# An encoder layer in split fp32: residual stage and first row of block products rearranged

## The chip, the cores and the metric

The kernel runs on one core of one Trainium2 chip. The metric is the device time of one execution in microseconds; the median of several executions is given. Engines are named as the profile names them: PE is TensorE's matmul, PEld its weight load, DVE is VectorE, ACT is ScalarE, POOL is GpSimd, SP is the sync engine, which here only issues transfers.

## The reference

One layer on x of 512 positions by 2048 channels, in fp32. Two mixers run on the normalised input, their outputs are concatenated and multiplied by `W_out`, and then the second half of the layer follows:

```python
x = x + rms_norm(concat(A, B) @ W_out, post_gain)         # residual 1
h = rms_norm(x, pre2_gain)
gate, val = split(causal_depthwise_conv(h @ W_up, conv_w), 2)   # three taps
x = x + rms_norm((gelu(gate) * val) @ W_down, post2_gain)
```

The change touches what lies between `concat(A, B) @ W_out` and the products with `W_up`.

## The kernel before

Activations are held transposed: channels on the 128 partitions, 512 positions along the row, so 2048 channels are 16 tiles of 128x512, indexed k. fp32 precision is kept by splitting every operand into a rounded part h (cast on ACT) and the remainder l (a subtraction on DVE); a product is then three matmuls, wh·xh, wh·xl and wl·xh. Weights arrive as `wraw` tiles of 128x1024 (512 KB, SP's queue, three buffers); ACT makes `wh` (L100) and DVE makes `wl` (L101), two buffers each in the pool `wp`. In `gemm` one weight tile feeds 24 matmuls of 512 columns, and eight such tiles (kc = 0 to 7) make one product with all 2048 channels.

The stretch in question, in program order:

- **Residual stage (L679 to L702).** `yt(k)` holds the mixer output, 16 tiles that lie in the two large buffers `yo` (in the rows these show as `s`). All 16 tiles of x were loaded earlier as `xin`. For each k, DVE multiplies `yt(k)` by the norm factor `ry` (L688), DVE adds the product to `xin` (L689), ACT makes the h part (L690), DVE the l part (L691), SP stores the sum to the scratch `x1scr` (L693), ACT squares it (L698), GpSimd adds the square to `ssq` (L699). ACT also writes the sum times its gain back into `yt(k)` (L702), for the block products later. The multiplication of k waits in order for the l part of k-3 (`issue_after`).
- **up(0) and up(1) (L735 to L746).** Two plain products of 2048 channels. PE starts on k = 0 while the residual stage runs, so the matmuls of up(0) follow the l parts. Where up(0) ends, DVE evacuates it (L741, four tiles, scaled by `r2`), scales the block operands by `r2` (L752, four large operations), runs the taps (L728) and forms the block operands (`xsum` L762, `xsplit` L767 to L771).
- **Rows of block products (L793 to L872).** Forty rows f. Each is a 2x2 block product done with seven products instead of eight: sums of weight blocks times sums of input blocks, 24 matmuls of 256 columns each. `quad_load` fetches the weight blocks. Two of them are sums, `s1` and `s3`: SP loads one block, and a transfer issued on GpSimd with `accum_op=ADD` adds the second (L820, L821). `s1`, `s3` and `rb` (block w22) come from the pool `sp`, which is opened where the pool of `yo` was closed and takes its place in memory; so the first loads into `sp` wait until the last reader of `yo`, the split "22" (L770, L771), is done. PE begins the first row with `product(s1, "t1")`.
- **down (from L906).** The product with `W_down`, whose inputs `hidh` (ACT) and `hidl` (DVE) are split in `fload`.

Instructions are put in order per engine by a list scheduler that goes by priority: program order, moved ahead by `tc.high_priority` with WPRI for weight work, EPRI for evacuations, and back with LPRI.

Of the kernel before, what the change touches and what calls it, by code (L numbers as in the profile page):

```python
# [10 lines left out]
F32 = mybir.dt.float32  # L11
I32 = mybir.dt.int32
F32R = mybir.dt.float32r
AF = mybir.ActivationFunctionType
ALU = mybir.AluOpType

P = 128
S = 512
D = 2048
DK = D // P  # L20
# [13 lines left out]
WPRI = 4000  # L34
# [3 lines left out]
LPRI = 30000  # L38
NP = 4
HS = S // 2  # L40

MAGIC = 12582912.0

# [11 lines left out]
MUL, ADD, SUB = ALU.mult, ALU.add, ALU.subtract  # L55
# [3 lines left out]
def layer_kernel(ctx, tc, a, out):  # L59
    nc = tc.nc  # L60
    ve, se, ge, pe, sy = nc.vector, nc.scalar, nc.gpsimd, nc.tensor, nc.sync
# [5 lines left out]
    wp = ctx.enter_context(tc.tile_pool(name="wp", side="right", bufs=2))  # L67
# [159 lines left out]
    g2 = cload("pre_ffn_g", [P, DK])  # L227
# [171 lines left out]
    for h in range(2):  # L399
        wc = s16.tile([P, 2, 16, P], F32, name="s16") if h == 0 else cv.tile([P, 2, 16, P], F32, name="csb")  # L400
        btw.append(wc)
        for j in range(T):
            sy.dma_start(out=wc[j:P:T],
                         in_=wscr[h][:, :, T - 1 - j, :].unsqueeze(0).broadcast_to([HC, 2, 16, P]))
        for mm in range(4):
            m = 4 * h + mm
# [13 lines left out]
    for m in range(8):  # L420
# [15 lines left out]
        for gg in range(2):  # L436
            sy.dma_start(out=cscr[m][:, :, gg].rearrange("r p q t -> p r q t"),
                         in_=ct[PH * gg:PH * gg + PH].rearrange("p r q t h -> p r q (t h)"))
# [44 lines left out]
    for ri in range(2):  # L483
        sy.dma_start(out=bst[PH * ri:PH * ri + PH, :, 0:NQ, :],
                     in_=bscr.rearrange("(g p) r q h -> r p g q h", p=PH)[ri])
# [95 lines left out]
    for m in range(8):  # L581
# [3 lines left out]
                         in1=yh[:, m, :].bitcast(F32).rearrange("p (c j) -> p c j", j=T), op=SUB)  # L585
# [6 lines left out]
    for g in range(2):  # L592
        ps = gemm(a["w_glu"][g], yrhs)
        for i in range(4):
            m = 4 * g + i
            with tc.high_priority(offset=EPRI):
# [4 lines left out]
                             in1=sg.rearrange("p (c j) -> p c j", j=T), op=MUL)  # L601
# [13 lines left out]
    for i in range(8):  # L615
# [3 lines left out]
        else:  # L619
            sq = tmp()  # L620
# [13 lines left out]
    xin = ExitStack()  # L634
    xip = xin.enter_context(tc.tile_pool(name="xin", bufs=1, reuse_waits="tile"))
    x1s = []
    for k in range(DK):
        x1 = xip.tile([P, S], F32, name=f"xin{k}")
        sy.dma_start(out=x1, in_=a["x"][:, k, :])
        x1s.append(x1)  # L640
# [4 lines left out]
    def yt(m):  # L645
        return yo[m // 8][:, m % 8, :]
# [10 lines left out]
    for g in range(4):  # L657
        ps = gemm(a["w_out"][1, g], crhs)
        for i in range(4):
            m = 4 * g + i  # L660
            with tc.high_priority(offset=EPRI if m < DK - 1 else LPRI):
                ve.tensor_tensor(out=yt(m), in0=ps[i], in1=yt(m), op=ADD)
                sq = yss if m == 0 else tmp()
# [8 lines left out]
    ry = rsqrt_bcast([yss] + last, D, False)  # L672
# [7 lines left out]
    xadds, xls = [], []  # L680
    xs2 = rp.tile([P, S], F32, name="ssq")
    for k in range(DK):
        x1 = x1s[k]
        h, l = hrhs[k]
        with ExitStack() as order:
            if k:
                order.enter_context(tc.issue_after(xadds[k - 1] if k < 3 else xls[k - 3]))
            ve.tensor_tensor(out=yt(k), in0=yt(k), in1=ry, op=MUL)  # L688
        xadds.append(ve.tensor_tensor(out=x1, in0=x1, in1=yt(k), op=ADD).ins)  # L689
        se.activation(out=h, in_=x1, func=AF.Copy, scale=g2[:, k:k + 1])  # L690
        xls.append(ve.scalar_tensor_tensor(out=l, in0=x1, scalar=g2[:, k:k + 1], in1=h.bitcast(F32),  # L691
                                           op0=MUL, op1=SUB).ins)
        sy.dma_start(out=x1scr[:, k, :], in_=x1)  # L693
        if k == 0:
            se.activation(out=xs2, in_=x1, func=AF.Square)
        else:
            sq = tmp()
            se.activation(out=sq, in_=x1, func=AF.Square)  # L698
            ge.tensor_tensor(out=xs2, in0=xs2, in1=sq, op=ADD)  # L699
    r2 = rsqrt_bcast([xs2], D)  # L700
    for k in range(DK):
        se.activation(out=yt(k), in_=x1s[k], func=AF.Copy, scale=g2[:, k:k + 1])  # L702
    xin.close()


    upx = ExitStack()
    xt = upx.enter_context(tc.tile_pool(name="xt", bufs=1, reuse_waits="tile"))
    tset = [[xt.tile([P, 8, HS], F32R, name=f"t{i}{p}") for p in "hl"] for i in range(3)]
    NA = 4
    abuf = [xt.tile([P, S + 2], F32, name=f"ab{i}") for i in range(NA)]  # L710
    for t in abuf:
# [37 lines left out]
    for i in range(2):  # L749
        for j in range(2):  # L750
            o = slice(HS * j, HS * j + HS)
            ve.tensor_tensor(out=yo[i][:, :, o], in0=yo[i][:, :, o],  # L752
                             in1=r2[:, o].unsqueeze(1).broadcast_to([P, 8, HS]), op=MUL)
    q11, q12 = yo[0][:, :, 0:HS], yo[0][:, :, HS:S]
# [9 lines left out]
    def xsplit(name, src, sign=1.0):  # L764
        h, l = xset[name]
        if sign > 0:
            se.copy(out=h, in_=src)  # L767
            ve.tensor_tensor(out=l, in0=src, in1=h.bitcast(F32), op=SUB)
        else:
            se.activation(out=h, in_=src, func=AF.Copy, scale=-1.0)  # L770
            ve.scalar_tensor_tensor(out=l, in0=src, scalar=-1.0, in1=h.bitcast(F32), op0=MUL, op1=SUB)  # L771
# [10 lines left out]
    for i in range(1, NP // 2):  # L782
        up(i)
    xsplit("11", q11)
    xsplit("21", q21)
    xsplit("t4", q12)
    xsplit("22", q22, -1.0)
    s16x.close()

# [2 lines left out]
    sp = spx.enter_context(tc.tile_pool(name="sp", side="right", bufs=1, reuse_waits="tile"))  # L792
    nw = [0]  # L793

    def product(raw, name, ps, first, last):
        pool = sp if nw[0] % 3 == 2 else wp
        nw[0] += 1
        h = pool.tile([P, 1024], F32R, name="wh")
        l = pool.tile([P, 1024], F32R, name="wl")
        with tc.high_priority(offset=WPRI):  # L800
            se.copy(out=h, in_=raw)  # L801
            ve.tensor_tensor(out=l, in0=raw, in1=h.bitcast(F32), op=SUB)  # L802
        h, l = (v.rearrange("p (k f) -> p k f", f=P) for v in (h, l))
        xh_, xl_ = xset[name]
        o = ps[:, 0:HS]
        for k in range(8):
            pe.matmul(o, h[:, k, :], xh_[:, k, :], start=first and k == 0, stop=False, skip_group_check=True)  # L807
            pe.matmul(o, h[:, k, :], xl_[:, k, :], start=False, stop=False, skip_group_check=True)  # L808
            pe.matmul(o, l[:, k, :], xh_[:, k, :], start=False, stop=last and k == 7, skip_group_check=True)  # L809

    def quad_load(f):
        src = a["ffn_w_quad"][f - NP]
        with tc.high_priority(offset=WPRI):
            s1 = sp.tile([P, 1024], F32, name="s1", bufs=2)
            sy.dma_start(out=s1, in_=src[2])
            s3 = sp.tile([P, 1024], F32, name="s3", bufs=2)
            sy.dma_start(out=s3, in_=src[0])
            w11 = wp.tile([P, 1024], F32, name="wraw", bufs=3)
            sy.dma_start(out=w11, in_=src[0])
            ge.dma_start(out=s1, in_=src[3], accum_op=ADD)  # L820
            ge.dma_start(out=s3, in_=src[2], accum_op=ADD)  # L821
            w12 = wp.tile([P, 1024], F32, name="wraw", bufs=3)
            sy.dma_start(out=w12, in_=src[1])
            w22 = sp.tile([P, 1024], F32, name="rb", bufs=2)
            sy.dma_start(out=w22, in_=src[3])
        return w11, w12, s3, w22, s1
# [14 lines left out]
    for f in range(NP, NFF):  # L841
        ws = quad_load(f)
        w11, w12, s3, w22, s1 = ws
# [51 lines left out]
    def fload(b):  # L895
        r = []
        for i in range(4):
            if b:
                t = hid.tile([P, S], F32, name="fin", bufs=6)
                sy.dma_start(out=t, in_=fscr[:, 4 * b + i, :])  # L900
            else:
                t = f0[i]
            h = hid.tile([P, S], F32R, name="hidh")
            se.copy(out=h, in_=t)  # L904
            l = hid.tile([P, S], F32R, name="hidl")
            ve.tensor_tensor(out=l, in0=t, in1=h.bitcast(F32), op=SUB)  # L906
            r.append((h, l))
        return r

# [113 lines left out]
```

## Time and profile before

| | us |
|---|---|
| median of 3 runs | 2112.39 |
| lowest and highest | 2111.09, 2114.02 |
| profiled execution, its own time | 2115.38 |
| span of the profiled execution | 2112.5 |
| PE busy | 1962.2 (93%) |
| DVE busy | 1518.5 (72%) |
| ACT busy | 829.3 (39%) |
| POOL busy | 364.9 (17%) |
| mean granted TensorE clock | 0.964 |

PE is busy for 93% of the span, so what a change can win lies in PE's pauses and in the stretches where the clock is at its lower level. The list of waits names each pause by the PE instruction that waited, the instruction that ended the wait, and the time; the timeline and the tables by stretch show what the other engines did meanwhile.

### The profile page before, as it was taken

To read this page: it belongs to the slowest core of one execution; us is meant where nothing else is said; L and a number is where in the kernel's file an instruction comes from. 1 tells how busy PE (TensorE), PEld (TensorE's weight loads), DVE (VectorE), ACT (ScalarE), POOL (GpSimd) and SP (SyncE) were. 2 spreads that over 40 slices of the span, in tenths; PEclk is the share of its full clock that TensorE was granted. 3 is DMA by queue.
4 is the path that set the end of the run, shared out by engine and by line. 5 is a ranking of instruction groups with operands and counts; after the bars stand their busy time and mean duration, and the time that the engine had idled before them with its cause. 6 is when DMAs were issued, how large, how long until landed. Compare 5 with 4: busy or idle time off the path is not lost. (4 is left out here: it accounts for less than half of the span.)

```text
span 2112.5 us, 30280 instructions
## 1 busy us (share of the span) xinstructions
PE 1962.2 (93%) x12070; PEld 1750.8 (83%) x12070; DVE 1518.5 (72%) x1945; ACT 829.3 (39%) x1050; POOL 364.9 (17%) x369
## 2 busy tenths in 40 slices
PE   7777998799998859999999999999998999999995
PEld 6656787677786749999999999999997888888884
DVE  6398999999538977778787787877874455555546
ACT  5111233433546444444444444444444322222223
POOL 6664144402123100000000000000000000000004
PEclk9979999999998979999999999999999999999997
DMA  6675576322523356776767767667655343333222
GB/s 209 184 218 162 192 206 197 93 90 90 179 95 111 106 164 190 203 192 193 209 184 197 202 193 205 185 197 207 186 150 209 120 134 118 118 120 122 98 100 90
DMA packets 141357, 338.79 MB, mean 160 GB/s; under 512 B 31393, under 2 KB 52897, under 8 KB 140705
## 3 DMA queue, kind: packets, MB, share of 16 engines
q1 hardware_dynamic: 124944, 292.82, 41.4%
q0 software_dynamic: 11520, 41.95, 11.6%
q10 hardware_dynamic: 4752, 2.11, 0.5%
q8 instruction: 94, 1.54, 0.3%
q14 instruction: 47, 0.38, 0.1%
HBM read 304.12 MB, written 32.70 MB: 159 GB/s over the span
## 5 line engine op out<-in xcount | busy, mean ns | idle before, releaser
L101 DVE TENSOR_TENSOR wl<-wraw,wh 128x1024 fp32r<-128x1024 f32 (+1 forms) x193 | 254.5, 1319 | 235.5 <-ACT wh L100 229.1
L100 ACT CAST wh<-wraw 128x1024 fp32r<-128x1024 f32 (+1 forms) x193 | 202.0, 1047 | 500.6 <-PE mm L121 457.6
L122 PE MATMUL mm<-hl,wl 128*128 128x512 f32 x832 | 313.8, 412 | 59.7 <-DVE wl L101 59.6
L807 PE MATMUL mm<-hl,wh 128*128 128x256 f32 x1280 | 362.5, 283 | 1.6 <-ACT wh L801 1.0
L808 PE MATMUL mm<-hl,wh 128*128 128x256 f32 x1280 | 362.3, 283 | 0.0
L809 PE MATMUL mm<-hl,wl 128*128 128x256 f32 x1280 | 362.1, 283 | 0.0
L120 PE MATMUL mm<-hl,wh 128*128 128x512 f32 x832 | 335.4, 406 | 18.3 <-ACT wh L100 11.3
L121 PE MATMUL mm<-hl,wh 128*128 128x512 f32 x832 | 333.9, 403 | 0.3 <-DVE hl L691 0.3
L120 PE MATMUL mm<-hidh,wh 128*128 128x512 f32 x704 | 274.9, 391 | 5.4 <-ACT hidh L904 5.4
L121 PE MATMUL mm<-hidl,wh 128*128 128x512 f32 x704 | 274.6, 390 | 0.0
L122 PE MATMUL mm<-hidh,wl 128*128 128x512 f32 x704 | 258.2, 390 | 0.0
L122 PEld LDWEIGHTS mm<-hl,wl 128*128 128x128 f32 x832 | 164.4, 198 | 106.4 <-DVE wl L101 71.0
L807 PEld LDWEIGHTS mm<-hl,wh 128*128 128x128 f32 x1280 | 245.9, 192 | 2.0 <-ACT wh L801 1.2
L808 PEld LDWEIGHTS mm<-hl,wh 128*128 128x128 f32 x1280 | 245.9, 192 | 0.0
L809 PEld LDWEIGHTS mm<-hl,wl 128*128 128x128 f32 x1280 | 245.8, 192 | 0.0
L802 DVE TENSOR_TENSOR wl<-s,wh 128x1024 fp32r<-128x1024 f32 x120 | 146.8, 1223 | 100.5 <-ACT wh L801 100.5
L120 PEld LDWEIGHTS mm<-hl,wh 128*128 128x128 f32 x832 | 163.2, 196 | 54.1 <-ACT wh L100 12.7
L801 ACT CAST wh<-s 128x1024 fp32r<-128x1024 f32 x120 | 126.2, 1051 | 191.4 <-DVE s L858 92.0
L801 ACT CAST wh<-wraw 128x1024 fp32r<-128x1024 f32 x120 | 126.2, 1052 | 184.4 <-PE mm L808 184.4
L121 PEld LDWEIGHTS mm<-hl,wh 128*128 128x128 f32 x832 | 162.8, 196 | 36.8 <-DVE hl L691 1.2
L571 DVE SCALAR_TENSOR_TENSOR csb<-z,c_conv_w,csb 128x512 f32<-128x512 f32 x210 | 179.0, 910 | 2.0 <-ACT csb L564 1.9
L802 DVE TENSOR_TENSOR wl<-wraw,wh 128x1024 fp32r<-128x1024 f32 x120 | 146.7, 1222 | 28.2 <-ACT wh L801 25.2
(268 smaller groups left out, 3574.1 us busy)
## 6 DMA issues: line engine op xcount, KB each, us to landing
wraw<-in_ffn_w_down SPq DMA_DIRECT2D x88, 512.0 KB, 3.2
wraw<-in_ffn_w_quad SPq DMA_DIRECT2D x80, 512.0 KB, 4.3
s<-in_ffn_w_quad SPq DMA_DIRECT2D x80, 512.0 KB, 3.3
s<-in_ffn_w_quad POOLq DMA_DIRECT2D x80, 512.0 KB, 7.8
wraw<-in_w_in SPq DMA_DIRECT2D x47, 512.0 KB, 4.5
rb<-in_ffn_w_quad SPq DMA_DIRECT2D x40, 512.0 KB, 7.5
wraw<-in_w_out SPq DMA_DIRECT2D x32, 512.0 KB, 3.3
fscr<-tmp SPq DMA_DIRECT2D x44, 256.0 KB, 5.2
```

Source lines behind the costliest of these rows:

```text
L100: se.copy(out=h[:, o], in_=raw[:, o])
L101: ve.tensor_tensor(out=l[:, o], in0=raw[:, o], in1=h[:, o].bitcast(F32), op=SUB)
L120: pe.matmul(ps[m], wh[:, kk, m, :], xh, start=k == 0, stop=False)
L121: pe.matmul(ps[m], wh[:, kk, m, :], xl, start=False, stop=False)
L122: pe.matmul(ps[m], wl[:, kk, m, :], xh, start=False, stop=k == nk - 1)
L571: ve.scalar_tensor_tensor(out=csb[:, c, :], in0=zk, scalar=w, in1=csb[:, c, :], op0=MUL, op1=ADD)
L801: se.copy(out=h, in_=raw)
L802: ve.tensor_tensor(out=l, in0=raw, in1=h.bitcast(F32), op=SUB)
L807: pe.matmul(o, h[:, k, :], xh_[:, k, :], start=first and k == 0, stop=False, skip_group_check=True)
L808: pe.matmul(o, h[:, k, :], xl_[:, k, :], start=False, stop=False, skip_group_check=True)
L809: pe.matmul(o, l[:, k, :], xh_[:, k, :], start=False, stop=last and k == 7, skip_group_check=True)
```

## The change

- Only three tiles of x (`NX = 3`) are loaded ahead. For k of 3 and above the residual is added by a transfer that GpSimd issues with `accum_op=ADD`, 256 KB each, thirteen of them, straight into `yt(k)`; for the first three DVE adds as before. The sum stays in `yt(k)`; h, l, the store, the square and the scaling by the gain read it there (the scaling is in place, so it comes after the store).
- The multiplication of k follows the l part of k-6 instead of k-3.
- The 15 additions of squares go from GpSimd to DVE.
- The first row's `s1` and `s3` get tiles of their own (`s1a`, `s3a`) that do not lie in the place of `yo`.
- The split "t4" stands ahead of "21" in the program; in the rotation of product buffers the first one from `sp` is product 3 instead of 2; `fload`'s splits run at WPRI; the scratch for transfer descriptors is 4096 instead of the default.

```diff
+NX = 3
-    for k in range(DK):
+    for k in range(NX):
         x1 = xip.tile([P, S], F32, name=f"xin{k}")
         sy.dma_start(out=x1, in_=a["x"][:, k, :])
...
-        x1 = x1s[k]
+        x1 = yt(k)
...
-                order.enter_context(tc.issue_after(xadds[k - 1] if k < 3 else xls[k - 3]))
-            ve.tensor_tensor(out=yt(k), in0=yt(k), in1=ry, op=MUL)
-        xadds.append(ve.tensor_tensor(out=x1, in0=x1, in1=yt(k), op=ADD).ins)
+                order.enter_context(tc.issue_after(xadds[k - 1] if k < NX else xls[max(k - 6, 0)]))
+            m = ve.tensor_tensor(out=x1, in0=x1, in1=ry, op=MUL).ins
+        if k < NX:
+            m = ve.tensor_tensor(out=x1, in0=x1, in1=x1s[k], op=ADD).ins
+        else:
+            ge.dma_start(out=x1, in_=a["x"][:, k, :], accum_op=ADD)
+        xadds.append(m)
...
-            ge.tensor_tensor(out=xs2, in0=xs2, in1=sq, op=ADD)
+            ve.tensor_tensor(out=xs2, in0=xs2, in1=sq, op=ADD)
...
-        se.activation(out=yt(k), in_=x1s[k], func=AF.Copy, scale=g2[:, k:k + 1])
+        se.activation(out=yt(k), in_=yt(k), func=AF.Copy, scale=g2[:, k:k + 1])
...
+    s13 = [xt.tile([P, 1024], F32, name=f"s{i}a") for i in (1, 3)]
...
+    xsplit("t4", q12)
     xsplit("21", q21)
-    xsplit("t4", q12)
...
-        pool = sp if nw[0] % 3 == 2 else wp
+        pool = sp if nw[0] and nw[0] % 3 == 0 else wp
...
-            s1 = sp.tile([P, 1024], F32, name="s1", bufs=2)
+            s1 = s13[0] if f == NP else sp.tile([P, 1024], F32, name="s1", bufs=2)
...
-            s3 = sp.tile([P, 1024], F32, name="s3", bufs=2)
+            s3 = s13[1] if f == NP else sp.tile([P, 1024], F32, name="s3", bufs=2)
...
-            se.copy(out=h, in_=t)
...
-            ve.tensor_tensor(out=l, in0=t, in1=h.bitcast(F32), op=SUB)
+            with tc.high_priority(offset=WPRI):
+                se.copy(out=h, in_=t)
+                ve.tensor_tensor(out=l, in0=t, in1=h.bitcast(F32), op=SUB)
...
-    nc = bacc.Bacc("TRN2", target_bir_lowering=False, num_devices=1)
+    nc = bacc.Bacc("TRN2", target_bir_lowering=False, num_devices=1, dynamic_dma_scratch_size=4096)
```

Lines of the changed kernel are six or seven higher than those of before from L640 on. How the instructions then stand, at the places that matter:

GpSimd, from the residual stage to the second row of block products, before (`ssq` is the sum of squares, `s_5806` and `s_5808` are the first row's `s1` and `s3`, `s_5968` the second row's `s1`):

```order
L699 TENSOR_TENSOR ssq<-ssq,tmp 128x512 x15
L712 MEMSET ab_5231 128x2
...
L820 DMA s_5806<-in_ffn_w_quad 128x1024
L821 DMA s_5808<-in_ffn_w_quad 128x1024
L820 DMA s_5968<-in_ffn_w_quad 128x1024
```

The same stretch of GpSimd after (`s_3917` and `s_3918` are the two halves of `yt`, `s_5942` is the second row's `s1`):

```order
L693 DMA s_3917<-in_x 128x512 x4
L718 MEMSET ab_5207 128x2
...
L693 DMA s_3917<-in_x 128x512
L826 DMA s1a<-in_ffn_w_quad 128x1024
L693 DMA s_3918<-in_x 128x512
L827 DMA s3a<-in_ffn_w_quad 128x1024
L693 DMA s_3918<-in_x 128x512 x7
L826 DMA s_5942<-in_ffn_w_quad 128x1024
```

The additions are gone from GpSimd, thirteen accumulating transfers stand there, and the first row's two stand among them instead of behind the stage.

DVE, from the last weight split ahead of up(0)'s evacuation to the next one, before:

```order
L101 TENSOR_TENSOR wl<-wraw,wh 128x1024
L741 TENSOR_TENSOR ab_5231<-mm,rr 128x512
...
L752 TENSOR_TENSOR s_3943<-s_3943,rr 128x8x256 x2
L752 TENSOR_TENSOR s_3944<-s_3944,rr 128x8x256 x2
L101 TENSOR_TENSOR wl<-wraw,wh 128x1024
```

And after:

```order
L102 TENSOR_TENSOR wl<-wraw,wh 128x1024
L747 TENSOR_TENSOR ab_5207<-mm,rr 128x512
...
L758 TENSOR_TENSOR s_3917<-s_3917,rr 128x8x256 x2
L758 TENSOR_TENSOR s_3918<-s_3918,rr 128x8x256 x2
L734 SCALAR_TENSOR_TENSOR tmp<-ab_5207,c_ffn_conv_w,tmp 128x512
...
L768 TENSOR_TENSOR s_3917<-s_3917 128x8x256
L102 TENSOR_TENSOR wl<-wraw,wh 128x1024 x2
```

One weight split more (kc = 1 of up(1)) stands ahead of the evacuation, and the next one (kc = 2) stands behind the four scalings, four taps and one block sum.

DVE at the start of the first row of block products, before:

```order
L768 TENSOR_TENSOR hl<-s_3944,hl 128x8x256
L728 SCALAR_TENSOR_TENSOR tmp<-ab_5231,c_ffn_conv_w,tmp 128x512
L771 SCALAR_TENSOR_TENSOR hl<-s_3944,hl 128x8x256
...
L802 TENSOR_TENSOR wl<-s_5806,wh 128x1024
L858 TENSOR_TENSOR s_5806<-s_5806,wraw 128x1024
L802 TENSOR_TENSOR wl<-s_5806,wh 128x1024
```

And after:

```order
L808 TENSOR_TENSOR wl<-s1a,wh 128x1024
L864 TENSOR_TENSOR s1a<-s1a,wraw 128x1024
L747 TENSOR_TENSOR ab_5207<-mm,rr 128x512
...
L808 TENSOR_TENSOR wl<-s1a,wh 128x1024
L774 TENSOR_TENSOR hl<-s_3918,hl 128x8x256
L734 SCALAR_TENSOR_TENSOR tmp<-ab_5207,c_ffn_conv_w,tmp 128x512
L777 SCALAR_TENSOR_TENSOR hl<-s_3918,hl 128x8x256
...
L808 TENSOR_TENSOR wl<-wraw,wh 128x1024
```

The first product's split stands ahead of up(1)'s evacuation, the second product's ahead of the splits "21" (L774) and "22" (L777), and the third's (`wraw`, block w11) behind them.

## Rows read from the trace of the kernel before

**Rows 1.** PE's waits, whole span: us in total, times, longest

```profile
PE mm L122 <- DVE wl L101: 59.6, 23, 10.7
PE mm L807 <- ACT wh L801: 24.8, 2, 23.8
```

**Rows 2.** PE's waits from 640 to 762 us

```profile
PE mm L122 <- DVE wl L101: 9.8, 4, 5.2
```

**Rows 3.** Timeline around the first block product: start us, us, engine, line, [idle before]

```profile
762.39 0.39 PE L122 MATMUL mm<-hl,wl 128*128 128x512 f32 x1
...
769.20 2.28 DVE L771 SCALAR_TENSOR_TENSOR hl<-s,hl 128x2048 fp32r<-128x2048 f32 x1
...
771.51 0.33 SPq L815 DMA_DIRECT2D s<-in_ffn_w_quad  x1
...
775.77 1.05 POOL L820 DMA_DIRECT2D s<-in_ffn_w_quad  x1 [72.56 <-DMA s<-in_ffn_w_quad]
776.58 1.15 POOL L821 DMA_DIRECT2D s<-in_ffn_w_quad  x1
...
785.47 1.05 ACT L801 CAST wh<-s 128x1024 fp32r<-128x1024 f32 x1 [8.94 <-DMA s<-in_ffn_w_quad]
...
786.57 0.58 PE L807 MATMUL mm<-t0h,wh 128*128 128x256 f32 x1 [23.79 <-ACT wh L801]
...
807.04 0.43 DVE L871 TENSOR_TENSOR ab<-mm,ab 128x256 f32<-128x256 f32 x1 [1.42 <-PE mm L809]
```

**Rows 4.** By stretch: us, PE, PEld, DVE, ACT, POOL busy (x), PEclk, DMA share, GB/s

```profile
680.00:700.00 20.00, 17.77 (x70) 14.22 (x71) 20.00 (x21) 13.02 (x20) 9.82 (x6) 0.91 0.42 150
740.00:760.00 20.00, 20.00 (x90) 16.57 (x89) 17.42 (x10) 9.40 (x7) 0.00 (x0) 1.00 0.44 141
780.00:800.00 20.00, 11.94 (x73) 11.44 (x73) 7.38 (x7) 5.29 (x6) 0.86 (x1) 0.66 0.91 230
820.00:840.00 20.00, 20.00 (x169) 20.00 (x168) 15.71 (x20) 9.66 (x12) 1.72 (x2) 1.00 0.70 196
```

**Rows 5.** Timeline of DVE, POOL and PE in the residual stage

```profile
655.78 2.08 PE L120 MATMUL mm<-hl,wh 128*128 128x512 f32 x4 [2.26 <-ACT hl L690]
656.81 0.75 DVE L691 SCALAR_TENSOR_TENSOR hl<-xin,c_pre_ffn_g,hl 128x512 fp32r<-128x512 f32 x1
657.48 0.68 DVE L688 TENSOR_TENSOR s<-s,aux 128x512 f32<-128x512 f32 x1
658.08 1.82 POOL L699 TENSOR_TENSOR ssq<-ssq,tmp 128x512 f32<-128x512 f32 x1 [29.13 <-ACT tmp L698]
658.67 1.77 DVE L691 SCALAR_TENSOR_TENSOR hl<-xin,c_pre_ffn_g,hl 128x512 fp32r<-128x512 f32 x1
...
685.60 2.32 DVE L101 TENSOR_TENSOR wl<-wraw,wh 128x1024 fp32r<-128x1024 f32 x1
```

**Rows 6.** Page, DMA queues: packets, MB, share of 16 engines; POOL's issues, us to landing

```profile
q1 hardware_dynamic: 124944, 292.82, 41.4%
q0 software_dynamic: 11520, 41.95, 11.6%
...
s<-in_ffn_w_quad POOLq DMA_DIRECT2D x80, 512.0 KB, 7.8
```

**Rows 7.** The tile s on POOL, all transfers

```profile
DMA to landing us min/median/max: 5.2/7.8/14.4
```

**Rows 8.** Timeline from the end of up(0) to the next weight split

```profile
711.59 2.48 DVE L741 TENSOR_TENSOR ab<-mm,rr 128x512 f32<-128x512 f32 x4 [4.17 <-ACT rr L152]
713.99 8.89 DVE L752 TENSOR_TENSOR s<-s,rr 128x2048 f32<-128x2048 f32 x4
722.79 1.22 DVE L101 TENSOR_TENSOR wl<-wraw,wh 128x1024 fp32r<-128x1024 f32 x1
723.93 2.73 DVE L728 SCALAR_TENSOR_TENSOR tmp<-ab,c_ffn_conv_w,tmp 128x512 f32<-128x512 f32 x4
724.06 0.80 PE L122 MATMUL mm<-hl,wl 128*128 128x512 f32 x1 [5.17 <-DVE wl L101]
```

## The prediction

> **What bounds the kernel now.** I read the list of PE's waits first. PE is busy 93% of the span, so a gain must come out of its pauses. Two groups matter here: 59.6 us on DVE's weight remainders (L101) and, in two waits, 24.8 us on the cast for the block products (L801), of which one wait is 23.8 [rows 1]. Of the 59.6 only 9.8 lies between 640 and 762 us, where the change works [rows 2]; the rest lies in stages whose order on PE, DVE, ACT and GpSimd is left as it was. So the change is worth some part of about 34 us plus what the low clock cost beside it.
>
> The timeline tells where the 23.8 us come from [rows 3]. The last matmul of up(1) ends at 762.39 + 0.39 = 762.8; call this moment U. The last split that reads `yo` ends at 771.5, only then SP issues the loads of `s1` and `s3`; GpSimd waits for them and issues its accumulating transfer at 775.8; it has landed at 785.5, ACT casts, and PE starts at 786.6. It is a chain of a freed buffer and two transfers in series. The product that ends the first row's first five is read by DVE at 807.0, that is U + 44.2.
>
> In the residual stage DVE is the bound: it is busy 20.00 of 20.00 us, PE 17.77 [rows 4]. An l part (L691) takes 0.75 us alone and 1.77 beside GpSimd's addition, a weight remainder 2.32 [rows 5] against 1.22 where GpSimd is idle [rows 8]. The Trainium skill says why ("SBUF — State Buffer", section "SBUF: two separate sides"): VectorE and GpSimd share a port pair, and who comes second is blocked; the trace agrees.
>
> **The change, part by part.** The sum goes against the profiled execution's own 2115.4 us, which is 3.0 over the median.
>
> *Residual stage.* Gone from DVE: 13 additions of 0.68 us and the slowdowns beside GpSimd. New on DVE: 15 additions of squares, of the same shape, some 0.7 us each. For two k DVE then does 2 multiplications (0.68), 2 l parts (0.75), 2 additions (0.7) and one remainder (1.22), 5.5 us at most as durations and less as pitch, since the starts of neighbours overlap by some 0.08 [rows 5]. PE needs 24 matmuls for the same, at 20.00/90 = 0.222 us [rows 4], 5.3 us. DVE and PE are about level, and neither waits on GpSimd's adds any more. Were PE never to wait, up(0)'s 192 matmuls, 42.7 us, with some 3 us more for the half clock in which the stage begins (0.52 us a matmul [rows 5]), would end at 655.8 + 45.7 = 701.5. Before, the evacuation begins at 711.6 [rows 8]. So at most 10 us are to be had.
>
> What can take them back is the DMA engines. The queue that GpSimd fills moved 41.95 MB in 11.6% of 2112.5 us, 171 GB/s; SP's 292.82 MB in 41.4%, 335 GB/s [rows 6]. An accumulating 256 KB costs 1.5 us of all 16 engines, a plain one 0.8. From about 659, when the first accumulating transfer is issued, to the landing of k = 15 the engines carry 13 x 1.5 = 20, two first-row sums of 512 KB accumulating (6.1) and plain (3.1), 14 stores (11) and some five weight tiles (7.8): 48 us if all went at these rates, 41 if they ran at the 85% that full queues may save (an estimate; the stretch 780 to 800, two thirds plain, shows 0.91 share at 230 GB/s [rows 4]). So k = 15 lands between 695 and 707, I take 700, and up(0) ends some 7 us behind it (h and l part 1.5, then 21 of the last tile's 24 matmuls, 4.7, and a little queueing): 707, with 701.5 and 714 as ends. Gain 4.6, from 10 down to a loss of 2.5. The issues cost GpSimd 0.9 to 1.1 us each [rows 3], covered, as it has nothing else to do. Two new waits stand in queues: on GpSimd the transfer into `s1a` waits for SP's load, issued between the stores of k = 1 and 2, and the transfers of k = 8 to 15 stand behind it; on DVE each l part from k = 3 waits for its transfer, and multiplications, square sums and weight remainders stand behind that. The multiplications run six ahead, some 16 us at PE's pace, which covers a landing of 7.8 [rows 7]; only if a landing nears 14.4 does DVE pass the wait on to PE.
>
> The Trainium skill ("DMA: Bandwidth & Descriptors", section "Anatomy of one DMA — SWDGE (gpsimd) path") gives 2.0 us plus bytes over 436 GB/s, an estimate of 2.6 us for 256 KB and 3.2 for 512 KB. Here accumulating 512 KB took 5.2 at least and 7.8 in the median [rows 7], so the measurement decides; by the page's price the stage would not be held by transfers and the sum would be about 5 us better.
>
> *up(1).* One more weight split stands ahead of the evacuation, but its buffers come free only with up(0)'s last matmul, so cast and remainder (2.3 us) go ahead of the evacuation. Then follow 2.48, 8.89, 2.73 [rows 8] and a block sum of 2.28, as the split of the same size [rows 3]. kc = 2's remainder is there some 20 us after up(0)'s end. PE has then done kc = 0 and 1, two tiles more or less as before one, and waits 6.5 to 8.5 us where it waited 5.2. I take 2 us of loss with what the clock costs: U stands 51.2 us behind up(0)'s end before (762.8 - 711.6), 53.2 after. U comes at 760.2, 2.6 earlier.
>
> *First row.* `s1a` and `s3a` do not lie in `yo`, and land some 50 us before they are wanted. The first product's split stands ahead of up(1)'s evacuation, so PE goes on at U without the 23.8 us. What is late next is DVE: after U it still has two evacuations (0.7 each), "t4", "21" and "22" (2.28 each), the second remainder (1.22), three to four taps (0.75) before the third product's remainder. The second product's remainder is ready at U + 4.7 (PE needs it at U + 3.1), the third's at U + 12.3 (needed at U + 7.7). With 24 x 20.00/169 = 2.84 us a product [rows 4], the third ends at U + 17 with 2 us for matmuls at half clock, as they follow the pauses of 2.26 and 23.79 us (0.52 a matmul of 512 columns [rows 5], granted clock 0.66 from 780 to 800 [rows 4]); then 2 matmuls of the next row's w11, which wait for their cast to U + 18.9; product four 21.7; the other 18 to 23.9 and product five at U + 26.5. Before it was U + 44.2. **Gain 17.7**; the floor, without any wait, is 140 matmuls or U + 16.6, the ceiling of trouble is below under the rivals.
>
> *Nothing each:* the square sums on GpSimd's side (covered above); fewer x loads, issued 80 us earlier into idle queues; the in-place scaling, which ACT does behind the store with 13.02 of 20 us busy [rows 4]; the rotation and the priority in `fload`, whose rows show almost the same order (at most 1 us either way); the smaller descriptor scratch, which makes GpSimd wait for a transfer five to seven back, three rows back in the steady rows.
>
> Sum: 2.6 + 17.7 = 20.3, less 0.4 for the steady rows' start. 2115.4 - 19.9 = 2095.5 on this execution, **2092.5** against the median. With the ends of the residual stage (+5.4, -7) it is 2087 to 2100.
>
> **The rivals.** (1) *More:* the transfers keep up and the stage is bound by PE (up(0) at 701.5, 5.5 us better), and the first row's pauses on DVE shrink by half of the 9.9 us between U + 26.5 and U + 16.6. 2092.5 - 5.5 - 5 = 2082. For it: the DMA share in the stage is 0.42 now [rows 4].
>
> (2) *The gap moves to the second row.* Its `s1`, `s3` and `rb` still wait for the split "22", now at U + 9.9. Before, the first sum was usable 14.0 us after that point (771.5 to 785.5 [rows 3]); then it would be at U + 24, wanted at about U + 32. But the longest transfer took 14.4 us to land [rows 7], and the second pair is issued some 5 us later; with loads of 5 and a landing of 14.4 on top it is U + 34 to 40, a wait of 5 to 12. 2092.5 + 5 to 12 = 2098 to 2105. Against: two loads and two accumulating transfers fewer compete.
>
> (3) *Slower: the accumulating transfers go one after the other.* If each begins only when the one before has landed, 15 of them at d us end at 659 + 15 d, up(0) 7 us later. The gain is gone when up(0) ends 15.7 us later than before (17.7 less 2), at 727.3, so from d = 4.1 us on. At 5.2 [rows 7] it is 744: 2112 + 17 = 2129; at 7.8, 2168. One thing could do that: GpSimd writes these transfers' descriptors, and DVE, busy 20.00 of 20.00, could hold it off. The skill has a rule of this kind (the same page on SBUF, same section, its box on the DVE-blocks-DMA trap): while VectorE runs certain two-port operations, GpSimd cannot write descriptors. Against it: two issued 0.8 us apart [rows 3] were in flight together, and the steady rows, with DVE busy 15.71 of 20, let two per row through without a wait of PE [rows 4].
>
> (4) *No change:* what the first row gains is lost in the residual stage: k = 15 at about 720, up(0) at 727, 2112.
>
> **How the numbers follow.** 0.2% is 4.2 us, about what a measurement of this kernel can tell from no change. Forecast, 2087 to 2098: 0.58. More, 2080 to 2087: 0.12. Second row, 2098 to 2106: 0.14. Within 0.2%: 0.06. Slower: 0.10, nearly all of it rival 3. The range 2081 to 2106 leaves out 0.18. Faster 0.84, same 0.06, slower 0.10.
>
> **What would show it.** In the changed profile PE's wait on the cast of `s` should shrink from 23.8 us to under 2, with the first block product right behind up(1); POOL should show transfers and no additions from 658 to 700, and l parts of 0.75 us throughout; the landing of 256 KB accumulating should be 2 to 6 us, DMA share above 0.8 from 660 to 700. up(0)'s evacuation should begin near 707, a wait of 6 to 9 us on L102 should stand in up(1), and one of some 5 us in the first row on L808's remainder of w11. Wrong if up(0) ends after 714, if PE waits over 3 us for `s` or `rb` in the second row, or if the steady rows, 20 us each, change their pace.

## The result, and the profile after

The changed kernel takes 2091.06 us (2089.16 to 2094.14, 4 runs) against 2112.2 for the kernel before; the ratio is 0.990 with a 95% interval of 0.9883 to 0.9918. The forecast was 2092.5. The profiled execution took 2092.54 us, its span is 2090.6.

PE's list of waits for the whole span shows where the time went (line waited at, releaser: us in total, times, longest). It answers to [rows 1]:

```profile
PE mm L123 <- DVE wl L102: 60.7, 19, 11.3
...
PE mm L815 <- DVE wl L808: 5.7, 2, 4.4
...
PE mm L813 <- ACT wh L807: 1.5, 1, 1.5
```

The two waits on the cast for block products, 24.8 us, have become one of 1.5 us, and two on DVE's remainders (L808), 5.7 us, are new. The waits on the remainders of plain weights stayed at about 60.

The timeline around the first block product (start, us, engine, line, [idle before]) answers to [rows 3]:

```profile
757.93 0.39 PE L123 MATMUL mm<-hl,wl 128*128 128x512 f32 x1
758.16 0.28 PE L813 MATMUL mm<-t0h,wh 128*128 128x256 f32 x1
...
762.71 0.39 PE L815 MATMUL mm<-t1h,wl 128*128 128x256 f32 x1 [1.28 <-DVE wl L808]
...
770.24 0.58 PE L815 MATMUL mm<-hl,wl 128*128 128x256 f32 x1 [4.39 <-DVE wl L808]
776.10 0.39 PE L813 MATMUL mm<-hl,wh 128*128 128x256 f32 x1 [1.47 <-ACT wh L807]
...
784.47 0.43 DVE L877 TENSOR_TENSOR ab<-mm,ab 128x256 f32<-128x256 f32 x1 [2.69 <-PE mm L815]
```

The first block product stands right behind up(1)'s last matmul, at U = 758.2. The fifth product is read at U + 26.3, where it was U + 44.2.

The residual stage by stretch (us, PE, PEld, DVE, ACT, POOL busy (x), PEclk, DMA share, GB/s) answers to [rows 4]:

```profile
660.00:680.00 20.00, 17.77 (x72) 14.23 (x71) 15.53 (x24) 14.57 (x23) 8.77 (x14) 0.91 1.08 247
680.00:700.00 20.00, 19.24 (x90) 15.72 (x89) 14.84 (x22) 17.37 (x27) 0.86 (x1) 1.00 0.93 280
```

DVE, busy 20.00 of 20 us before, has 15 now; the DMA engines, at a share of 0.42 before, are full. The issues from 655 to 710 us (out<-in, queue, count, KB, median us to landing) say what that does to a transfer:

```profile
wraw<-in_ffn_w_up SPq DMA_DIRECT2D x8, 512.0 KB, 11.3
x1scr<-s SPq DMA_DIRECT2D x14, 256.0 KB, 6.9
s<-in_x POOLq DMA_DIRECT2D x13, 256.0 KB, 10.6
```

The weight tiles of up(0) and up(1), and the stores of the stage, had landed sooner before (the same view of the kernel before, 575 to 790 us):

```profile
wraw<-in_ffn_w_up SPq DMA_DIRECT2D x16, 512.0 KB, 3.2
...
x1scr<-xin SPq DMA_DIRECT2D x16, 256.0 KB, 2.0
```

And the timeline of the stage, which answers to [rows 5]:

```profile
656.17 3.72 POOL L693 DMA_DIRECT2D s<-in_x  x4 [29.52 <-DVE s L689]
...
665.99 1.22 DVE L102 TENSOR_TENSOR wl<-wraw,wh 128x1024 fp32r<-128x1024 f32 x1
667.12 0.75 DVE L696 SCALAR_TENSOR_TENSOR hl<-s,c_pre_ffn_g,hl 128x512 fp32r<-128x512 f32 x1
...
674.28 1.76 PE L121 MATMUL mm<-hl,wh 128*128 128x512 f32 x4 [2.23 <-ACT wh L101]
```

An l part takes 0.75 us and a remainder 1.22 throughout: the slowdowns beside GpSimd's additions are gone. PE waits for a weight cast instead, 3.0 us in two waits. It is not the weight tile that is late: the tile of the longer wait is the fourth of up(0), and its load was issued at 640.63, 33 us ahead of the cast. It is ACT, where the cast stands behind an in-place scaling (L707), which has to wait until the store of the same data has landed (SP's queue, then ACT):

```profile
640.63 6.71 SPq L91 DMA_DIRECT2D wraw<-in_ffn_w_up  x2
...
672.58 0.72 ACT L707 ACTIVATE s<-s,c_pre_ffn_g 128x512 f32<-128x512 f32 x1 [3.34 <-DMA x1scr<-s]
673.21 1.03 ACT L101 CAST wh<-wraw 128x1024 fp32r<-128x1024 f32 x1
```

ACT's list of waits from 655 to 702 us has four of these:

```profile
ACT s L707 <- DMA x1scr<-s: 5.7, 4, 3.3
```

PE's second wait, 0.8 us before 693.3, is of the same kind: that tile's load was issued at 675.5 and landed 11.3 us later, and ACT, held up by a store until 689.0, came to it at 692.2. The granted clock was 0.58 from 674 to 678 us, after the longer wait.

The last of the thirteen accumulating transfers (k = 15) was issued on GpSimd at 682.24 and landed 9.6 us later, at 691.9. PE was behind its inputs by then: after the wait that ended at 693.3 it ran without a pause to the end of up(0).

From the end of up(0) on, answering to [rows 8]:

```profile
705.27 1.05 ACT L101 CAST wh<-wraw 128x1024 fp32r<-128x1024 f32 x1 [5.02 <-PE mm L122]
706.36 1.23 DVE L102 TENSOR_TENSOR wl<-wraw,wh 128x1024 fp32r<-128x1024 f32 x1 [4.52 <-ACT wh L101]
706.39 1.05 PE L149 MATMUL aux<-c_ident,rs 128*128 128x128 f32 x8
...
708.10 2.49 DVE L747 TENSOR_TENSOR ab<-mm,rr 128x512 f32<-128x512 f32 x4 [0.52 <-ACT rr L153]
710.50 8.89 DVE L758 TENSOR_TENSOR s<-s,rr 128x2048 f32<-128x2048 f32 x4
719.30 2.73 DVE L734 SCALAR_TENSOR_TENSOR tmp<-ab,c_ffn_conv_w,tmp 128x512 f32<-128x512 f32 x4
721.95 2.29 DVE L768 TENSOR_TENSOR s<-s 128x2048 f32<-128x2048 f32 x1
724.15 2.36 DVE L102 TENSOR_TENSOR wl<-wraw,wh 128x1024 fp32r<-128x1024 f32 x2
725.43 0.80 PE L123 MATMUL mm<-hl,wl 128*128 128x512 f32 x1 [6.39 <-DVE wl L102]
```

L149 makes the broadcast of the norm factor r2 on PE; ACT copies it (L153), and only then can DVE evacuate. In PE's order it stands behind five matmuls of up(1), so up(0)'s own last matmul ended at 706.39 - 5 x 0.2275 = 705.25 (0.2275 us is the distance of two matmuls in this timeline), and the evacuation began 2.9 us later. Most of this is DVE's own order: ahead of the evacuation it makes the remainder of up(1)'s second weight tile, whose cast waited for up(0)'s last matmuls (705.27, 706.36). Only the 0.52 us after it were a wait for r2.

That gives three stages to compare, free of what lies ahead of them: from the residual stage's first multiplication (L688, after L689) to up(0)'s last matmul; from there to up(1)'s last (U); from U to DVE's reading of the first row's fifth product.

| us | before | forecast | after |
|---|---|---|---|
| residual stage and up(0) | 57.9 | 53.4 | 54.0 |
| up(1) | 51.3 | 53.2 | 52.9 |
| U to the fifth product | 44.2 | 26.5 | 26.3 |
| sum | 153.4 | 133.1 | 133.2 |

Three stages gain 20.2 us of the 21.1 between the medians. The rest is not tied to the change: the first multiplication stood at 653.6 in the profile before and at 651.3 after, but in the profiles of the kernels below it stands anywhere from 650.2 to 654.5, though the order of the instructions that PE, DVE, ACT and GpSimd carry out ahead of it is the same in all; the changed kernel alone had it at 651.3 and, profiled a second time, at 651.7.

### The profile page after: what moved, and what is told of

It reads as the page before. It is cut to its first block, busy times and chain, and to the rows that moved or that the text cites. A ratio compares the mean times of both kernels' runs of the same rounds, so it can differ in the third digit from the quotient of the medians.

```text
span 2090.6 us, 30295 instructions
## 1 busy us (share of the span) xinstructions
PE 1956.1 (94%) x12070; PEld 1746.7 (84%) x12070; DVE 1506.4 (72%) x1947; ACT 827.8 (40%) x1050; POOL 343.8 (16%) x367
## 5 line engine op out<-in xcount | busy, mean ns | idle before, releaser
L102 DVE TENSOR_TENSOR wl<-wraw,wh 128x1024 fp32r<-128x1024 f32 (+1 forms) x193 | 251.0, 1301 | 243.1 <-ACT wh L101 237.8
L808 DVE TENSOR_TENSOR wl<-s,wh 128x1024 fp32r<-128x1024 f32 x117 | 143.2, 1224 | 87.5 <-ACT wh L807 87.5
L808 DVE TENSOR_TENSOR wl<-wraw,wh 128x1024 fp32r<-128x1024 f32 x120 | 146.7, 1223 | 24.8 <-ACT wh L807 21.9
```

The lines of the kernel that those rows point to most:

```text
L102: ve.tensor_tensor(out=l[:, o], in0=raw[:, o], in1=h[:, o].bitcast(F32), op=SUB)
```

## The experiments

**Theory A:** the first row's own homes carry most of the gain, by taking away the chain of freed buffer, load and accumulating load; the new residual stage carries little, because what DVE gains there is taken back by full DMA engines. **Rival B:** the residual stage carries it. **Rival C:** DVE, not the DMA engines, holds the residual stage. All stages of all kernels are in one table at the end of this section; the medians of a group below were taken on one chip, beside runs of the kernel before. That kernel's median was 2112.9 us beside experiments 1 to 4, 2113.0 beside 5 to 8 and 2114.5 beside 9 to 11, and the changed kernel was timed again only beside 9 to 11; so a difference of a microsecond or two between groups shows nothing.

**1. The homes undone.**

```diff
-            s1 = s13[0] if f == NP else sp.tile([P, 1024], F32, name="s1", bufs=2)
+            s1 = sp.tile([P, 1024], F32, name="s1", bufs=2)
```

(and s3 likewise)

> The changed kernel with one part undone: the first row's s1 and s3 come from the pool sp again. Theory A (the homes carry the gain, the new residual stage little): PE's wait on the cast of s comes back with 20 to 24 us, time 2107 to 2112. Rival B (the accumulating residual and the moved square sums carry the gain, the homes only shift a wait): the wait stays under 10 us, time under 2100.

2109.04 us. PE's timeline has the old wait back, at the old place:

```profile
780.69 0.58 PE L812 MATMUL mm<-t0h,wh 128*128 128x256 f32 x1 [23.41 <-ACT wh L806]
```

U to the fifth product is 43.3 us. So the homes are worth 18 us, and theory A holds on this point. The residual stage is 51.8 us without the two first-row sums among its transfers, 2.2 less than with them.

**2. The homes alone on the kernel before.**

```diff
-            s1 = sp.tile([P, 1024], F32, name="s1", bufs=2)
+            s1 = s13[0] if f == NP else sp.tile([P, 1024], F32, name="s1", bufs=2)
```

(s3 likewise, the product rotation, and `dynamic_dma_scratch_size=4096`, without which the tiles do not fit)

> The kernel before with the homes alone (s1a, s3a, the product rotation and the smaller descriptor scratch that makes room for them); residual added by DVE, squares on GpSimd. Theory A: first block product right behind up(1), time 2091 to 2096. Rival B: above 2102.

2095.28 us. The residual stage is that of before (57.9), U to the fifth product 28.1. From both sides the parts add up: the homes 17.6 to 18 us, all the rest 3.9 (2112.92 - 2109.04) to 4.2 (2095.28 - 2091.06, which are of two groups).

**3. No accumulating transfer of x: all 16 tiles loaded ahead, added by DVE.**

```diff
-NX = 3
+NX = 16
```

> The changed kernel with all 16 tiles of x loaded ahead and added by DVE, no accumulating transfer of x. Theory A with the DMA engines as what holds the residual stage (share 1.08 and 0.93 there): share falls under 0.5 from 680 to 700, DVE's 13 more additions fit at about 6.1 us for two k, up(0) ends 2 to 5 us earlier, time 2086 to 2090. Rival C (DVE holds the stage): the additions lengthen it, time 2092 to 2097.

2092.88 us, so the time fits rival C; the stages do not. The DMA share is 0.53 and 0.65 (above the 0.5 expected for the second), PE has no wait there from 655 to 680 us, and up(0) ends 49.7 us after the first multiplication, the shortest of all kernels here:

```profile
660.00:680.00 20.00, 20.00 (x90) 16.57 (x89) 20.00 (x31) 16.17 (x25) 0.00 (x0) 1.00 0.53 171
680.00:700.00 20.00, 19.08 (x82) 14.88 (x81) 17.28 (x25) 12.70 (x20) 1.77 (x2) 1.00 0.65 212
```

Of the 4.3 us by which that is shorter, 0.8 have only moved: the eight small products of r2's square sum (L136), inside up(0) in the changed kernel, stand behind three matmuls of up(1) here. The other 3.5 us are lost behind the stage. r2's broadcast now stands behind 24 matmuls of up(1) in PE's order, and DVE waits for it, so the evacuation begins no earlier:

```profile
700.53 0.95 PE L136 MATMUL aux<-ones,ssq 128*128 128x1 f32 x8
...
707.95 1.29 DVE L747 TENSOR_TENSOR ab<-mm,rr 128x512 f32<-128x512 f32 x2 [4.19 <-ACT rr L153]
```

up(1) takes 56.6 us instead of 52.9 and the first row 28.2 instead of 26.3. Theory A was right on what held the stage, and the forecast of the time wrong, because it stopped at the end of the stage.

**4. The square sums back on GpSimd.**

```diff
-            ve.tensor_tensor(out=xs2, in0=xs2, in1=sq, op=ADD)
+            ge.tensor_tensor(out=xs2, in0=xs2, in1=sq, op=ADD)
```

> The changed kernel with the 15 square sums back on GpSimd, between its transfers. If the DMA engines hold the stage, DVE's slower operations (l parts of 1.8 us beside an addition) are covered in part: 2091 to 2094. If DVE holds it, or the transfers are issued late behind additions: 2095 to 2100.

2094.15 us, at the edge between the two; the stage tells more. DVE's groups from 655 to 705 us (busy, mean ns | idle before) have the l part at 1352 ns instead of 748:

```profile
L696 DVE SCALAR_TENSOR_TENSOR hl<-s,c_pre_ffn_g,hl 128x512 fp32r<-128x512 f32 x15 | 20.1, 1352 | 6.2 <-ACT hl L695 6.2
```

The residual stage is 57.5 us, as long as before the change. So nearly all that the stage gained came from moving 15 additions off GpSimd, not from the accumulating transfers: DVE has less to do where it does the additions itself (10.3 us of additions, against 9.1 us more in these 15 l parts and 3.9 more in seven remainders). That the additions delay GpSimd's issues is no rival: the last accumulating transfer is issued 32.0 us after the first multiplication, in the changed kernel 31.0, and of PE's 6.2 us of waits from 655 to 705 us 4.7 are for l parts and remainders on DVE.

**5. The first row's sums behind the residual stage.** Their loads are queued behind the last store, their accumulating transfers behind the last one of x.

```diff
+            with ExitStack() as order:
+                if f == NP:
+                    order.enter_context(tc.issue_after(xst[-1]))
+                sy.dma_start(out=s1, in_=src[2])
+                sy.dma_start(out=s3, in_=src[0])
```

> The changed kernel with the loads and accumulating transfers of s1a and s3a issued behind the last x1scr store and the last accumulating transfer of x. If the DMA engines hold the residual stage, taking 3 MB moved out of it ends up(0) some 2 us earlier after the stage's first multiplication (51.8 us instead of 54.0, as in the kernel without homes), and everything behind is as before: 2088 to 2090. If something else holds it, the same 54.0 and 2091. If the transfers come too late for the first block product, a wait on the cast of s1a.

The stage is 51.4 us, 2.6 shorter, as in the kernel without homes: the two sums cost that much in the full DMA engines. ACT's scalings wait 0.7 us for stores instead of 5.7, and the weight tiles land after 6.0 us instead of 11.3:

```profile
wraw<-in_ffn_w_up SPq DMA_DIRECT2D x8, 512.0 KB, 6.0
s<-in_x POOLq DMA_DIRECT2D x13, 256.0 KB, 8.2
```

up(1) gives 1.1 us back (54.0), and the median, 2091.11, does not show what is left. The first row did not wait for the later transfers.

**6. DVE's order in the first row.** The first row's five products are written ahead of the splits that they do not need yet; `sub` is the remainder of w11, then that of w12, then that of s3a.

```diff
+    with tc.issue_after(sub):
+        xsplit("21", q21)
...
+    with tc.issue_after(sub):
+        xsplit("22", q22, -1.0)
...
+    with tc.issue_after(sub):
+        xsplit("t4", q12)
+        gated(NP - 1, uab[2:4])
```

> The changed kernel with DVE's order in the first row changed: all five first products have their buffers in wp and their splits ahead of what is not yet needed; the split 21 follows the remainder of w11, 22 that of w12, t4 and the second pair of taps of up(1) that of s3a. If DVE's order, not a transfer, makes the first row's waits (1.3, 4.4 and 1.5 us in the changed kernel), they go, the fifth product is read at U + 18 to 21 instead of U + 26.3, time 2084 to 2087. If the second row's transfers then wait longer for 22, a new wait in the second row and 2088 to 2092.

2093.2 us, and U + 24.5 instead of 26.3: mostly a miss. The waits on DVE fell from 5.7 to 1.2 us, but PE's waits from 755 to 800 us now name ACT:

```profile
PE mm L809 <- ACT wh L803: 3.7, 3, 3.2
PE mm L809 <- ACT ab L834: 1.3, 1, 1.3
PE mm L811 <- DVE wl L804: 1.2, 2, 0.8
```

The first row is held by two engines in turn, and clearing one brings up the other.

**7. Both of the last two.**

> Both of the last two edits together. If they act in different stretches the gains add: 2082 to 2085.

2090.58 us, a miss and no gain on the changed kernel: 52.0 us for the stage, 53.8 for up(1), 25.1 for the first row. The sum of the three is 2.3 us shorter, too little for these medians.

**8. Multiplications three ahead instead of six.**

```diff
-                order.enter_context(tc.issue_after(xadds[k - 1] if k < NX else xls[max(k - 6, 0)]))
+                order.enter_context(tc.issue_after(xadds[k - 1] if k < NX else xls[k - 3]))
```

> The changed kernel with the multiplications three k ahead instead of six (as in the kernel before). The transfers of 256 KB land 10.6 us after issue in the median; three k are 8 us at PE's pace, so the l parts should wait for transfers and the residual stage should grow from 54.0 by 2 to 8 us, time 2093 to 2099. If the run ahead does not matter (the DMA engines' volume alone sets the pace): 54 to 55 us and 2091.

2097.45 us, but not for the reason given: the stage is 54.5, half a microsecond longer. The time is lost in the first row, at U + 30.5. ACT's timeline there:

```profile
760.97 1.91 ACT L773 CAST hl<-s 128x2048 fp32r<-128x2048 f32 x1 [1.09 <-PE mm L123]
762.79 1.90 ACT L776 ACTIVATE hl<-s 128x2048 fp32r<-128x2048 f32 x1
764.60 1.88 ACT L773 CAST hl<-s 128x2048 fp32r<-128x2048 f32 x1
766.38 0.72 ACT L732 ACTIVATE tmp<-ab,c_ffn_conv_w 128x512 f32<-128x512 f32 x1
767.01 1.03 ACT L807 CAST wh<-s1a 128x1024 fp32r<-128x1024 f32 x1
```

In the changed kernel the same cast of `s1a` comes before the last two of the three 1.9 us splits:

```profile
758.19 1.05 ACT L807 CAST wh<-s1a 128x1024 fp32r<-128x1024 f32 x1 [0.56 <-PE mm L122]
759.15 1.90 ACT L773 CAST hl<-s 128x2048 fp32r<-128x2048 f32 x1
760.94 1.91 ACT L776 ACTIVATE hl<-s 128x2048 fp32r<-128x2048 f32 x1
```

An edit in the residual stage changed the list scheduler's order on ACT 100 us later, and PE waits 4.3 us for the cast:

```profile
768.09 0.58 PE L813 MATMUL mm<-t1h,wh 128*128 128x256 f32 x1 [4.28 <-ACT wh L807]
```

The same wait stands in experiment 3's first row.

**9. The changed kernel again, beside a version that uses what the runs showed.**

> The changed kernel itself, timed on the same chip as the two that follow, and a second profile of it: 2089 to 2093; its stages should repeat within a few tenths (residual stage 54.0 us from the first multiplication to up(0)'s last matmul, first row's fifth product at U + 26.3), while the moment of that first multiplication, ahead of all that the change touches, may again differ by 2 us or so.

2092.0 us; stages 54.1, 53.3, 26.3. The stages repeat within 0.4 us.

**10. Earlier r2, and block operands formed piece by piece.** On top of experiment 7:

```diff
-        ps = gemm(a["ffn_w_up"][i], hrhs)
+        ps = gemm(a["ffn_w_up"][i], hrhs, use=use, behind=((28 + 0, norm_mm[-5]), (28 + 2, norm_mm[-1])) if i == 0 else ((0, norm_mm[-1]),))
...
+    def prep(kc):
+        if kc < 2:
+            return
+        with tc.issue_after(subs[-1]):
+            if kc == 2:
+                xsum(q12, q12, q11)
+                yscale(1)
...
```

`behind` keeps up(0)'s last matmuls, and all of up(1), behind r2's two small products; `prep` is called by `gemm` ahead of each weight split of up(1), and its work follows the split before.

> The edits of e7 and two more: the two small products of r2 stand earlier in PE's order (behind kc = 6 and in the middle of kc = 7 of up(0), ahead of up(1)), and the block operands are formed piece by piece behind the weight splits of up(1). If DVE's work from up(0)'s evacuation to the first row is what PE waits for, the evacuation begins 2 to 4 us earlier, the wait of 6.4 us in up(1) falls under 3, up(1) takes 47 to 50 us instead of 52.9 and the time is 2081 to 2086. If the work is bounded by its sum on DVE and not by its order, the wait only moves to a later tile or into the first row, and the time stays at 2088 to 2091.

2086.99 us (2083.94 to 2087.88), 5.0 under the changed kernel on the same chip; against the kernel before the ratio is 0.9871 (0.9856 to 0.9886), where the changed kernel has 0.9896 (0.9881 to 0.9911). The evacuation starts 50.5 us after the first multiplication instead of 56.9, and the next weight split no longer stands behind all four scalings:

```profile
700.94 1.29 DVE L757 TENSOR_TENSOR ab<-mm,rr 128x512 f32<-128x512 f32 x2 [2.42 <-ACT rr L163]
702.14 4.48 DVE L770 TENSOR_TENSOR s<-s,rr 128x2048 f32<-128x2048 f32 x2
...
709.07 1.22 DVE L104 TENSOR_TENSOR wl<-wraw,wh 128x1024 fp32r<-128x1024 f32 x1
710.20 4.49 DVE L770 TENSOR_TENSOR s<-s,rr 128x2048 f32<-128x2048 f32 x2
```

PE's wait in up(1) is 3.3 us instead of 6.4, and up(1) takes 47.5 us instead of 52.9; up(1) came as expected, the wait and the time missed their ranges by less than 1 us, and the evacuation came earlier than expected. Part of up(1)'s gain is the clock: the granted clock was 0.50, the lower level, from 724 to 728 us in the changed kernel, behind the wait of 6.4, and stays at 1.00 behind the wait of 3.3. So it was the order on DVE and PE, not the sum of DVE's work, that kept up(1) long; which of the two edits counts for how much was not run.

**11. The same without accumulating transfers of x** (`NX = 16`).

> The same with all 16 tiles of x loaded ahead and added by DVE, so without accumulating transfers of x. By the theory that these transfers hold the residual stage through the DMA engines, the stage takes 50 to 51 us and, now that r2's products are not queued behind up(1), the 3 us stay in the time: 2 to 4 us under the kernel before it in this list. By the rival that DVE's additions cost what the transfers save, within 1 us of it.

2092.03 us, 5 slower than experiment 10: neither reading. (Two things differ besides `NX`: r2's products stand one group of six matmuls later in up(0), and the first row's accumulating transfers are not held behind those of x, as there are none.) The stage is 52.1 us against 52.4, so its transfers cost little once the first row's sums are out of it. up(1) takes 50.5 us against 47.5: PE's wait is 4.0 us instead of 3.3, and the granted clock is 0.50 from 720 to 724 us, where it was 1.00. And the first row takes 29.7 us, with ACT's three splits ahead of the cast of `s1a` once more (a wait of 4.3 us). Whether NX = 16 would win with ACT's order kept is open; it was not run.

The stages of all kernels, in us. The first column is the time of the residual stage's first multiplication, the last the median.

| | first mult. | residual, up(0) | up(1) | U to fifth | median |
|---|---|---|---|---|---|
| before | 653.6 | 57.9 | 51.3 | 44.2 | 2112.2 |
| after | 651.3 | 54.0 | 52.9 | 26.3 | 2091.1 |
| 1 no homes | 652.4 | 51.8 | 53.1 | 43.3 | 2109.0 |
| 2 homes only | 654.5 | 57.9 | 51.2 | 28.1 | 2095.3 |
| 3 NX = 16 | 650.2 | 49.7 | 56.6 | 28.2 | 2092.9 |
| 4 squares on GpSimd | 650.7 | 57.5 | 54.8 | 26.4 | 2094.2 |
| 5 sums late | 653.9 | 51.4 | 54.0 | 26.4 | 2091.1 |
| 6 first row's order | 651.7 | 54.0 | 52.7 | 24.5 | 2093.2 |
| 7 both | 653.4 | 52.0 | 53.8 | 25.1 | 2090.6 |
| 8 three ahead | 653.6 | 54.5 | 52.7 | 30.5 | 2097.5 |
| 9 after again | 651.7 | 54.1 | 53.3 | 26.3 | 2092.0 |
| 10 staged | 650.4 | 52.4 | 47.5 | 25.1 | 2087.0 |
| 11 staged, NX = 16 | 651.5 | 52.1 | 50.5 | 29.7 | 2092.0 |

## Why the prediction was right

- **The bound.** The wait on the cast of `s` was where the time lay; it went from 23.8 us to none, and came back whole when the homes were undone (experiment 1). Shown.
- **The first row.** What was late next was DVE, at the places named: the second product's remainder (a wait of 1.28 us, forecast 1.6 by U + 4.7 against U + 3.1) and the third's (4.39, forecast some 4.6). The wait of 1.47 us on ACT's cast is the one that the prediction has before two matmuls of the next row's w11; it ended at U + 17.9, forecast U + 18.9. The fifth product came at U + 26.3, forecast 26.5. So the mechanism held here wait by wait. What the prediction did not price is that ACT is the second bound of this stretch, as the experiments showed.
- **up(1).** A wait of 6.39 us on L102, forecast 6.5 to 8.5; the stage 52.9, forecast 53.2. As forecast, one weight split went ahead of the evacuation, and the third tile's remainder stood ready 20.1 us behind up(0)'s end, forecast some 20. Experiment 10 shows that the order on DVE and PE makes the wait.
- **Residual stage.** 54.0, forecast 53.4, and the DMA engines were full as said (1.08 and 0.93). But the path to the number was another, and that it fits so well is luck. The forecast had k = 15 land at 700 on the clock of before, 695 at the earliest, and up(0) end 7 us behind it. The transfer landed at 691.9, on that clock 694.2, and up(0) ended 13.4 us behind it: two misses of about 6 us that cancel. The saving of 15% in full queues did not follow from its row either: two thirds at 335 GB/s and one third at 171 make 231 at a share of 0.91, which is what the row has, so it shows none. What put PE behind is a term that the prediction set at nothing, the in-place scaling behind the store: stores landed after 6.9 us instead of 2.0, ACT waited 5.7 us for them, and the weight casts behind ACT's scalings made PE wait 3.0. The waits are in the trace; that PE would gain them back with the scaling elsewhere was not run. Landing was forecast at 2 to 6 us and took 4.8 to 15.2, 10.6 in the median; the l parts still hardly waited for it. On the clock of before the evacuation began at 710.4 rather than near 707, the sign named; but the prediction's own sum for up(1) has the 2.3 us of a weight split ahead of it, and that, with 0.5 us of waiting for r2, is the difference from up(0)'s end.
- **What the stage owes to which edit.** The prediction put the gain down to the additions taken from DVE and the slowdowns beside GpSimd together. Experiments 3 and 4 separate them: moving the square sums is worth about 3.5 us of stage, and the accumulating transfers by themselves save nothing; with the first row's sums beside them they cost 3.5.
- **The rivals.** The transfers did not go one after the other: in the median each took 10.6 us to land, far above the 4.1 from which rival 3 was to decide, yet thirteen of them and the first row's two were through in 36 us (the first issued at 656.2, the last landed at 691.9). GpSimd's issues took 0.86 to 1.83 us with DVE busy three quarters of the time. The box on the DVE-blocks-DMA trap (the Trainium skill, "SBUF — State Buffer", section "SBUF: two separate sides") speaks of two-port perf-mode operations on VectorE; this mix of DVE operations did not hold GpSimd's transfers off, and no run here shows the operations that it names. The second row's transfers cost PE no wait: none for `s` or `rb` stands between 776 us and the end of the rows.
- **Small terms.** The wait at the start of down went from 5.4 to 4.6 us, inside the 1 us that was allowed; the priority in `fload` is not shown to be the cause, since experiment 2, which lacks it, has 4.6 as well. From the fifth product to the first matmul of down the changed kernel was 1.9 us shorter and from there to the end of the span 2.6 longer; neither was followed up.

## What to carry to other kernels

A pool that takes the place of another passes the last reader's lateness on to its first loads; a home of its own for the first iteration alone can be worth more than anything inside the loop, if the memory can be found. Price a stage to the moment at which its consumer really starts: in experiment 3, 3.5 us won in a stage were lost again behind a small product that stood late in an engine's order. Ask of an operation made in place what must be done with the old data first: here a scaling had to wait for a store, and weight casts that had nothing to do with it stood behind. And when a scheduler sets the orders, compare all engines' orders far behind the edit, for an unrelated edit moved ACT's by 4 us.

## What the runs showed of the hardware that was not expected

- An accumulating transfer of 256 KB took 10.6 us to land in the median beside stores and weight loads (8.2 without the first row's sums in the stage), while fifteen such transfers, two of them of 512 KB, passed in 36 us. The landing time says little of the throughput.
- Plain transfers on SP's queue suffered too: loads of 512 KB took 3.2 us before, 11.3 in the full stage and 6.0 with the two sums moved out, stores of 256 KB 2.0, 6.9 and 5.9.
- GpSimd's addition of 128x512 (1.82 us in [rows 5]) doubles what DVE's l parts and remainders take beside it (0.75 to 1.77, 1.22 to 2.32), and all of the stage's gain could be undone by putting it back (57.5 us against 57.9 before).
